# Two blocks of an output projection multiplied as a pair, with two of eight steps by seven products instead of eight

## The chip, the cores and the metric

The kernel runs on one core of one Trainium2 chip. The metric is the device time of the kernel in microseconds (us), the median of several runs. All data are float32.

## The reference

One layer of a hybrid decoder for 256 tokens of 2048 features. Two attention branches run on the same input, A (latent attention) and B (sliding window). Their outputs go through projections of their own, are gated, added and projected again; a gated feed-forward part follows. The part that matters here:

```python
merged = g[:, :, 0] * (o_a @ w_o_mla) + g[:, :, 1] * (o_b @ w_o_swa)
y = merged @ w_out
x = x + rms_norm(y, norm_mix_post)
```

`o_a` is 256 x 2048, `w_o_mla` and `w_out` are 2048 x 2048, `norm_mix_post` is the scale of 2048 numbers, and `g` are sigmoids of gate values.

## The kernel before, in words

**Products.** A float32 product is made of three matmuls in a reduced float32 type: every operand is split into a high and a low part, and `mm3` (L174) adds high by high, high by low and low by high into one PSUM bank (L175 to L177; the bank is 128 tokens by 512 columns). Activations stay in SBUF as pairs of tiles; two ktiles (128 rows of the contraction each) share one tile, so a product over 2048 rows has 16 ktiles in 8 ktile pairs. `AH`, `AL` are branch A's output (tiles `bhl0` to `bhl7`), `MH_`, `ML_` the merged values (`ahl0` to `ahl7`).

**Weights.** SP loads a chunk of 128 x 1024 into `raw` (up to five in flight), ScalarE casts it to the high part (`whi`, L143) and VectorE subtracts to get the low part (`wlo`, L144). High and low parts have rings of four buffers, so a conversion starts when TensorE has done with the chunk four before. `gemm` (L179) multiplies one block of 512 columns: 8 chunks of two ktiles, 12 matmuls each, with the two token halves in two banks.

**Pairs.** `pair_gemm` (L205) multiplies two blocks (1024 columns) at once into four banks, c11, c12, c21, c22 (token half by block). A "plain" ktile pair is multiplied as `gemm` would do it: 4 banks x 2 ktiles x 3, so 24 matmuls over two rows of weights of 1024 columns. A "seven" treats the 2 x 2 x 2 blocks of token halves, ktiles and column blocks by a scheme with seven products instead of eight: VectorE forms four sums of activation blocks (`token_sums`, L276) and four sums of weight blocks (L232 to L235), four of the products go to banks of their own (q1, q5, q7, q6), and behind the last seven VectorE adds these into four tiles d0 to d3 (L255 to L261), which the caller adds to c11 to c22. The two rows of weights of a seven are loaded by POOL's queue (L227, L228), the plain ones by SP's (L151). The kernel already multiplies a pair of gate blocks (`gate_pair`, L724, three sevens) and three pairs of the feed-forward part in this way.

**Steps.** Work that isn't on the main line is put on a calendar: `at(t, f)` runs f when `tick()` has counted t chunks; a scheduler then fixes the order on each engine. Each engine and each queue runs its instructions in order.

**Around the change.** Behind branch A's attention the four blocks of its gate were stored to DRAM (`ta_d`, L904) by POOL's queue, as were the gated blocks of branch B (`yb_d`). The loop at L950 to L958 then does, for each of four blocks j: POOL loads gate part `lta` (3 buffers) and `lyb` (2 buffers) from DRAM, one tile for each token half; `gemm` multiplies the block; VectorE merges, first (gate + 1) x product (L955), then + branch B (L956); and some chunks later TensorE transposes the merged block (`m_cols`, L930, tiles `mT`), which ScalarE and VectorE split into `ahl`. The accumulators come from the pool `pacc`, four banks taken in turn. The scale `gpost` (L917, L922) and the residual `x2` (L925) are loaded by SP during this loop, from chunk 10 on. The output product (L1013) follows, four blocks, of which the first uses the merged ktiles in order; `y_evac` (L969) reads the scale at L973. Two pools are opened ahead of the loop (`p6`, L916, and `px`, L927) over memory that the gate tiles (`ta`, `tb`) held.

Of the kernel before, what the change touches and what calls it, by code (L numbers as in the profile page):

```python
# [11 lines left out]
F32 = mybir.dt.float32  # L12
F32R = mybir.dt.float32r
# [3 lines left out]
ALU = mybir.AluOpType  # L17
AX = mybir.AxisListType

P = 128  # L20
D = 2048
S = 256
NT = 2
KT = D // P
# [17 lines left out]
def trunk_layer(ctx, tc, x, x_cols_in, conv_cols_in, g_mix_post, g_ffn_post, w_in, w_q, w_kv,  # L42
                sinks, rel, wo_a, wo_b, w_out, w_up, w_down, rope_tab, strip_sel, out):
    nc = tc.nc
    vec, act, pe, pool = nc.vector, nc.scalar, nc.tensor, nc.gpsimd
# [7 lines left out]
    pss = ctx.enter_context(tc.tile_pool(name="pss", bufs=2, space=PS))  # L53
# [5 lines left out]
    def sb(pl, shape, name, dt=F32, tag=None, bufs=None):  # L59
        return pl.tile(shape, dt, name=name, tag=tag or name, **({"bufs": bufs} if bufs else {}))  # L60
# [118 lines left out]
    def gemm(xh, xl, w, k0, nk, c0, n, split=None, extra=None, ps=None):  # L179

        kc = 1024 // n if n in (256, 512) else 2
        acc = new_acc("g", ps)
        todo = []
        cuts = list(range(0, nk, kc)) + [nk]
        for ci, (k, ke) in enumerate(zip(cuts[:-1], cuts[1:])):
            kk = ke - k
            src = w[(k0 + k) * P:(k0 + k + kk) * P, c0:c0 + n].rearrange("(a p) n -> p a n", p=P)
            hi, lo = wchunk(src, [kk, n], *(extra or {}).get(ci, ()))
            for j in range(kk):
                kt = k + j  # L190
# [473 lines left out]
    acc, _ = gemm(XH, XL, w_in, 0, KT, 0, 512)  # L664
# [4 lines left out]
    acc, _ = gemm(XH, XL, w_in, 0, KT, C_KV, KVR + ROPE)  # L669
# [21 lines left out]
    ta_d = dram.tile([4, NT, P, 512], F32, name="ta_d")  # L691
    yb_d = dram.tile([4, NT, P, 512], F32, name="yb_d")
# [55 lines left out]
    AH, AL = pair_view(ath), pair_view(atl)  # L748
# [138 lines left out]
    b = now[0] + 26  # L887
# [9 lines left out]
    at_ = [slot("b", p) for p in range(8)]  # L897
    ath[:], atl[:] = highs(at_), lows(at_)
    for j in range(4):
        acc, _ = gemm(XH, XL, w_in, 0, KT, C_GA + 512 * j, 512)  # L900
# [13 lines left out]
    x2_all = [sb(p3, [P, D], f"x2_{t}") for t in range(NT)]  # L914
    x2 = [[x_[:, j * 512:(j + 1) * 512] for j in range(4)] for x_ in x2_all]
    es6, p6 = open_pool("p6")  # L916
    gpost = sb(p6, [P, D], "gpost", tag="gp")  # L917

    def late_loads(i):

        if i < 4:
            nc.sync.dma_start(gpost[:, i * 512:(i + 1) * 512], g_mix_post[i * 512:(i + 1) * 512].partition_broadcast(P))  # L922
        else:
            t, j = divmod(i - 4, 4)
            nc.sync.dma_start(x2[t][j], x[t * P:(t + 1) * P, j * 512:(j + 1) * 512])  # L925

    esx, px = open_pool("px", bufs=EXTRA)  # L927
    es4, p4 = open_pool("p4")

    def m_cols(p, ld):  # L930
        pt = pst.tile([P, 512], F32, name=f"mT{p}", tag="t")
        for i in range(2):
            for t in range(NT):
                c = (2 * (p % 2) + i) * P
                pe.transpose(pt[:, i * 256 + t * P:i * 256 + (t + 1) * P], ld[t][0][:, c:c + P], ident)
        split_to(mth[p][:, :], mtl[p][:, :], pt, 0.5)

    def merge_loads(j):
        ld = []
        for t in range(NT):  # L940
            a = sb(p4, [P, 512], f"lta{j}_{t}", tag="lta", bufs=3)
            b = sb(p4, [P, 512], f"lyb{j}_{t}", tag="lyb", bufs=2)
            pool.dma_start(a, ta_d[j, t])
            pool.dma_start(b, yb_d[j, t])
            ld.append((a, b))
        return ld

    for i in range(12):
        at(now[0] + 10 + 2 * i, lambda i=i: late_loads(i))
    for j in range(4):  # L950
        ld = merge_loads(j)
        acc, _ = gemm(AH, AL, wo_a, 0, KT, 512 * j, 512)
        for t in range(NT):
            a, b = ld[t]
            vec.scalar_tensor_tensor(a, a, 1.0, acc[t], op0=ALU.add, op1=ALU.mult)  # L955
            vec.tensor_tensor(a, a, b, op=ALU.add)  # L956
        for p in range(2):
            at(now[0] + (3 if j == 3 else 1) + p, lambda p=2 * j + p, ld=ld: m_cols(p, ld))  # L958


    yg_all = [[sb(p6, [P, 1024], f"yg_{t}_{j}", tag="f" + "ab"[t], bufs=2) for j in range(2)] for t in range(NT)]
    yg = [[yg_all[t][j // 2][:, (j % 2) * 512:(j % 2 + 1) * 512] for j in range(4)] for t in range(NT)]
# [6 lines left out]
    def y_evac(acc, b, t):  # L969
        c0, n = W_BLOCKS[b]  # L970
        j, o = c0 // 512, c0 % 512
        act.activation(jk(f"yj{b}_{t}")[:, :n], acc[t][:, :n], AF.Square, accum_out=ssy[t][:, b:b + 1])
        vec.tensor_tensor(yg[t][j][:, o:o + n], acc[t][:, :n], gpost[:, c0:c0 + n], op=ALU.mult)  # L973

    x2hl = [slot("b", p) for p in range(8)]
    HH, HL = pair_view(highs(x2hl)), pair_view(lows(x2hl))
# [36 lines left out]
    for b in range(4):  # L1013
        c0, n = W_BLOCKS[b]
        last = b == 3
        acc, todo = gemm(MH_, ML_, w_out, 0, KT, c0, n, split=0 if last else None, extra={i: (px,) for i in range(EXTRA)} if last else None)
# [263 lines left out]
    ud = []  # L1280
# [5 lines left out]
    def pair_end(i):  # L1286
# [10 lines left out]
    for j in range(2, 4):  # L1297
        last = j == 3
        acc, todo = down(24, 20, 512 * j, 512, split=5 if last else None, ps=None if last else (pss, "s"))
# [25 lines left out]
RING = 4  # L1325
GATE_ORDER = "psppspsp"
B_ORDER = "pppsppspsp"
PAIR_ORDER = ("psppsppsppsp", "ppsppsppsppp")
XCUT = [0, 1, 2, 3, 4, 6, 8, 10, 12, 14, 16]
X_LOAD = [0, 1, 2, 3, 4, 6, 7, 8, 10]  # L1330
# [72 lines left out]
```

## Time and profile before

| what | value |
|---|---|
| time, median of 3 runs | 1468.54 us (1467.81 to 1469.31) |
| the profiled execution: its own time | 1470.05 us |
| its span, first to last instruction | 1468.3 us |
| TensorE busy | 1456.9 us, 99% |
| VectorE busy | 1067.2 us, 73% |
| ScalarE busy | 830.5 us, 57% |
| DMA | 287.60 MB, 196 GB/s on average |
| chain that ended last | TensorE 97% |

The profile is of one execution. Times in its rows count from the start of the span. A row of the timeline has the start, the duration, the engine, the line of the kernel, the operation, and the tiles (output<-inputs) without their numbers; in brackets stands how long the engine was idle before, and what ended that. Matmuls are pipelined: the duration of one holds its latency, and the distance of two starts says what it costs. PE is TensorE, PEld its weight load, DVE VectorE, ACT ScalarE; SPq is the DMA queue of SP.

### The profile page before, as it was taken

Reading aid. Unit: us, or ns where it says so; the run is one execution under the profiler, and the core shown is the slowest. Engines: PE = TensorE matmul, PEld = TensorE weight load, DVE = VectorE, ACT = ScalarE, POOL = GpSimd, SP = SyncE. Lnnn points to the kernel's source line nnn. Section 1 sums busy time; section 2 is a strip of 40 time slices with the busy share of each in tenths; the row PEclk is TensorE's granted clock in tenths of the full one; section 3 lists DMA queues with packets and bytes.
Section 4 is the critical chain, followed back from the end, with each engine's and each line's share of the span. In section 5 each row is a group of like instructions: output and inputs, shape, how many; then the busy total and the mean of one; then the engine's idle time right before and its main releaser. Section 6 shows DMA issues by size and latency. Waiting matters only on the chain.

```text
span 1468.3 us, 20938 instructions
## 1 busy us (share of the span) xinstructions
PE 1456.9 (99%) x7576; PEld 1244.8 (85%) x7576; DVE 1067.2 (73%) x1881; ACT 830.5 (57%) x1372; POOL 64.9 (4%) x113
## 2 busy tenths in 40 slices
PE   9999999999999999999999999999999999999997
PEld 7888888888888888888888888888888888888886
DVE  7688896745667665555699976778776687677775
ACT  7588874543555554444566655555454565555453
POOL 0011110000000000000000000000000000000000
PEclk9999999999999999999999999999999999999999
DMA  8755376466655559756766666665656666667573
GB/s 297 211 164 167 108 259 192 162 212 200 191 156 160 164 163 334 226 184 212 225 205 185 188 193 193 187 187 187 218 174 213 198 187 189 187 197 233 163 237 129
DMA packets 149909, 287.60 MB, mean 196 GB/s; under 512 B 18428, under 2 KB 29597, under 8 KB 149677
## 3 DMA queue, kind: packets, MB, share of 16 engines
q1 hardware_dynamic: 141312, 256.80, 56.5%
q0 software_dynamic: 8400, 29.41, 6.4%
q8 instruction: 59, 0.97, 0.3%
q14 instruction: 46, 0.37, 0.1%
q10 hardware_dynamic: 92, 0.05, 0.0%
HBM read 277.79 MB, written 8.44 MB: 195 GB/s over the span
## 4 chain that ended last, share of the span: by engine, by line
PE 97%; DVE 2%; ACT 1%; issue 0%; DMA 0%; DVEq 0%; ACTq 0%
PE accg L175 13%; PE accg L177 13%; PE accg L176 13%; PE ub L1147 10%; PE ua L1147 10%; PE ua L1151 5%; PE ub L1151 5%; PE cd L177 2%; PE cd L175 2%; PE cd L176 2%; PE cdb L175 1%; PE cdb L177 1%; PE cdb L176 1%; PE mpo L875 1%; PE cg L176 1%; PE cg L177 1%
## 5 line engine op out<-in xcount | busy, mean ns | idle before, releaser
L144 DVE TENSOR_TENSOR wlo<-raw,whi 128x1024 fp32r<-128x1024 f32 (+2 forms) x476 | 576.3, 1214 | 282.5 <-ACT whi L143 275.2
L143 ACT CAST whi<-raw 128x1024 fp32r<-128x1024 f32 (+2 forms) x476 | 494.7, 1043 | 427.5 <-PE accg L177 172.3
L175 PE MATMUL accg<-whi,ahl 128*128 128x512 f32 (+1 forms) x480 | 187.9, 392 | 0.0
L177 PE MATMUL accg<-whi,ahl 128*128 128x512 f32 (+1 forms) x480 | 185.6, 387 | 0.0
L176 PE MATMUL accg<-wlo,ahl 128*128 128x512 f32 (+1 forms) x480 | 184.8, 385 | 0.0
L1147 PE MATMUL ua<-ahl,whi 128*128 128x512 f32 x640 | 154.6, 391 | 0.0
L1147 PE MATMUL ub<-ahl,whi 128*128 128x512 f32 x640 | 154.6, 391 | 0.0
L175 PE MATMUL accg<-whi,bhl 128*128 128x512 f32 x378 | 148.2, 392 | 0.0
L177 PE MATMUL accg<-whi,bhl 128*128 128x512 f32 x378 | 147.4, 390 | 0.0
L176 PE MATMUL accg<-wlo,bhl 128*128 128x512 f32 x378 | 147.3, 390 | 0.0
L1147 PEld LDWEIGHTS ub<-ahl,whi 128*128 128x128 f32 x640 | 117.5, 188 | 22.9 <-ACT cc L1045 0.2
L1147 PEld LDWEIGHTS ua<-ahl,whi 128*128 128x128 f32 x640 | 117.6, 188 | 22.7
L177 PEld LDWEIGHTS accg<-whi,ahl 128*128 128x128 f32 x480 | 90.1, 188 | 18.0
L176 PEld LDWEIGHTS accg<-wlo,ahl 128*128 128x128 f32 x480 | 90.3, 188 | 15.6
L175 PEld LDWEIGHTS accg<-whi,ahl 128*128 128x128 f32 x480 | 90.3, 188 | 15.5
L1151 PEld LDWEIGHTS ub<-ahl,wlo 128*128 128x128 f32 x640 | 82.2, 191 | 3.2
L1151 PEld LDWEIGHTS ua<-ahl,wlo 128*128 128x128 f32 x640 | 82.2, 191 | 3.1
L1151 PE MATMUL ua<-ahl,wlo 128*128 128x256 f32 x640 | 83.7, 283 | 0.0
L177 PEld LDWEIGHTS accg<-whi,bhl 128*128 128x128 f32 x378 | 71.0, 188 | 14.8
L176 PEld LDWEIGHTS accg<-wlo,bhl 128*128 128x128 f32 x378 | 71.0, 188 | 14.5
L1151 PE MATMUL ub<-ahl,wlo 128*128 128x256 f32 x640 | 83.2, 283 | 0.0
L175 PEld LDWEIGHTS accg<-whi,bhl 128*128 128x128 f32 x378 | 71.0, 188 | 14.3
(545 smaller groups left out, 2218.9 us busy)
## 6 DMA issues: line engine op xcount, KB each, us to landing
raw<-in_ffn_w_up_dram SPq DMA_DIRECT2D x176, 512.0 KB, 4.5
raw<-in_w_in_dram SPq DMA_DIRECT2D x105, 512.0 KB, 4.5
raw<-in_ffn_w_down_dram SPq DMA_DIRECT2D x68, 512.0 KB, 4.5
raw<-in_w_o_swa_dram SPq DMA_DIRECT2D x32, 512.0 KB, 4.4
raw<-in_w_o_mla_dram SPq DMA_DIRECT2D x32, 512.0 KB, 4.5
raw<-in_w_out_dram SPq DMA_DIRECT2D x32, 512.0 KB, 4.1
bias<-strip POOLq DMA_DIRECT2D x16, 256.0 KB, 4.4
raw<-in_mla_w_q_up_dram SPq DMA_DIRECT2D x32, 128.0 KB, 2.8
```

What stands on the lines that cost most here:

```text
L143: act.copy(hi[:, a:b], raw[:, a:b])
L144: vec.tensor_tensor(lo[:, a:b], raw[:, a:b], hi[:, a:b].bitcast(F32), op=ALU.subtract)
L175: pe.matmul(o, ah, bh, start=start, stop=False)
L176: pe.matmul(o, ah, bl, start=False, stop=False)
L177: pe.matmul(o, al, bh, start=False, stop=stop)
L875: pe.matmul(o, w(t), p_[:, c], start=n == 0, stop=n == 5)
L1147: pe.matmul(acc[i], hi[:, c], hn[p][:, j * 512:(j + 1) * 512], start=p + j == 0, stop=stop)
L1151: pe.matmul(acc[i][:, 0:256], lo[:, c], hn[p][:, j * 512:j * 512 + 256], start=False, stop=False)
```

## The change

Blocks 1 and 2 of branch A's projection are multiplied as a pair; blocks 0 and 3 stay single. `A_ORDER` has the sevens at the fourth and the seventh place of eight; they take ktile pairs 0 and 1, so the plain ones begin with pair 2. The token sums are made during block 0 (calendar 1 and 4). The two sevens' weights go into the scale's tile and into `px`, and the scale is loaded during block 3 instead of from chunk 10 on. `lta` has a fourth buffer. The first parts `lta` of both blocks are loaded ahead of the pair, `lyb` of block 1 too, and `lyb` of block 2 in a step of its own, one chunk into block 3. At the pair's end VectorE adds each c to its d and merges. Block 3 takes its accumulators from the pool `pss`, whose banks q1 and q5 had.

```diff
     es6, p6 = open_pool("p6")
-    gpost = sb(p6, [P, D], "gpost", tag="gp")
+    gpost = []
...
         if i < 4:
-            nc.sync.dma_start(gpost[:, i * 512:(i + 1) * 512], g_mix_post[i * 512:(i + 1) * 512].partition_broadcast(P))
+            if i == 0:
+                gpost.append(sb(p6, [P, D], "gpost", tag="gp"))
+            nc.sync.dma_start(gpost[0][:, i * 512:(i + 1) * 512], g_mix_post[i * 512:(i + 1) * 512].partition_broadcast(P))
...
-    def merge_loads(j):
+    def merge_loads(j, kinds="ab"):
...
+            for kind, tag, src, bufs in (("a", "lta", ta_d, 4), ("b", "lyb", yb_d, 2)):
+                if kind in kinds:
+                    both.append(sb(p4, [P, 512], f"{tag}{j}_{t}", tag=tag, bufs=bufs))
+                    pool.dma_start(both[-1], src[j, t])
...
-    for i in range(12):
-        at(now[0] + 10 + 2 * i, lambda i=i: late_loads(i))
-    for j in range(4):
+    as_ = {}
+
+    def a_sums(u):
+        st = sb(px, [P, 1024], f"as{u}", F32R, tag="w" + ("hi", "lo")[u % 2])
+        tmp = sb(p6, [P, 1024], f"at{u}", tag="f" + "ab"[u % 2], bufs=2)
+        as_[u] = token_sums(at_[u].bitcast(F32), tmp[:, 0:512], tmp[:, 512:1024], st[:, 0:512], st[:, 512:1024])
+
+    def merged(a, b, acc):
+        vec.scalar_tensor_tensor(a, a, 1.0, acc, op0=ALU.add, op1=ALU.mult)
+        vec.tensor_tensor(a, a, b, op=ALU.add)
...
+    def a_place():
+        a_done[0] += 1
+        i = a_done[0]
+        if i % 2:
+            both = sb(p6, [P, D], f"ar{i}", tag="gp")
+            return both[:, 0:1024], both[:, 1024:2048]
+        return [sb(px, [P, 1024], f"ar{i}{n}", tag="w" + n) for n in ("hi", "lo")]
...
+    def f_pair(name):
+        return [sb(p6, [P, 1024], f"{name}{n}{cnt[0]}", tag="f" + n, bufs=2) for n in "ab"]
...
+    def single(j):
         ld = merge_loads(j)
-        acc, _ = gemm(AH, AL, wo_a, 0, KT, 512 * j, 512)
+        acc, _ = gemm(AH, AL, wo_a, 0, KT, 512 * j, 512, ps=(pss, "s") if j == 3 else None)
         for t in range(NT):
-            a, b = ld[t]
-            vec.scalar_tensor_tensor(a, a, 1.0, acc[t], op0=ALU.add, op1=ALU.mult)
-            vec.tensor_tensor(a, a, b, op=ALU.add)
+            merged(*ld[t], acc[t])
...
+    def a_pair():
+        lds = [merge_loads(1), merge_loads(2, "a")]
+        c = pair_gemm("a", wo_a, 0, 512, A_ORDER, lambda k, t: (AH(k)[:, t * P:(t + 1) * P], AL(k)[:, t * P:(t + 1) * P]),
+                      lambda u: as_[u], 0, ud_place, a_place, lambda: f_pair("ta"))
+
+        def pair_evac(i):
+            t, j = divmod(i, 2)
+            vec.tensor_tensor(ud_a[i], ud_a[i], c[i], op=ALU.add)
+            merged(*lds[j][t], ud_a[i])
+
+        def second_b():
+            for t, (b,) in enumerate(merge_loads(2, "b")):
+                lds[1][t].append(b)
+
+        for n_, i in zip((0, 1, 3, 4), (0, 2, 1, 3)):
+            at(now[0] + n_, lambda i=i: pair_evac(i))
+        at(now[0] + 1, second_b)
+        for p in range(2, 6):
+            at(now[0] + 1 + p, lambda p=p: m_cols(p, lds[p // 2 - 1]))
+
+    for u in range(A_ORDER.count("s")):
+        at(now[0] + 1 + 3 * u, lambda u=u: a_sums(u))
+    for i in range(4, 12):
+        at(now[0] + 10 + 2 * i, lambda i=i: late_loads(i))
+    single(0)
+    a_pair()
+    for i in range(4):
+        at(now[0] + i, lambda i=i: late_loads(i))
+    single(3)
...
+A_ORDER = "pppsppsp"
```

How this moves instructions, at the three places that the prediction speaks of. First VectorE's queue in block 0, before: the conversions of block 0's last chunks (353 to 361) and of block 1's first (363 to 367) stand next to each other, then come the merges.

```order
L144 TENSOR_TENSOR wlo_5930<-raw_5927,whi_5929 128x1024
L144 TENSOR_TENSOR wlo_5948<-raw_5945,whi_5947 128x1024
L144 TENSOR_TENSOR wlo_5966<-raw_5963,whi_5965 128x1024
L144 TENSOR_TENSOR wlo_5984<-raw_5981,whi_5983 128x1024
L144 TENSOR_TENSOR wlo_6002<-raw_5999,whi_6001 128x1024
L144 TENSOR_TENSOR wlo_6034<-raw_6031,whi_6033 128x1024
L144 TENSOR_TENSOR wlo_6052<-raw_6049,whi_6051 128x1024
L144 TENSOR_TENSOR wlo_6077<-raw_6074,whi_6076 128x1024
L955 SCALAR_TENSOR_TENSOR lta_0_5863<-lta_0_5863,accg_346_0_5871 128x512
```

The same place now, the beginning (the first token sum, L278 to L284, in tiles `at0` and `as0`, and the second in `at1`) and the end (the weight sums of the second seven, L232 to L235, and the first merge, now L959):

```order
L144 TENSOR_TENSOR wlo353_5938<-raw352_5935,whi353_5937 128x1024
L278 TENSOR_TENSOR at0_5909<-bhl0_4096 128x512
L144 TENSOR_TENSOR wlo355_5956<-raw354_5953,whi355_5955 128x1024
L281 TENSOR_TENSOR at0_5909<-at0_5909 128x128
...
L144 TENSOR_TENSOR wlo363_6057<-raw362_6054,whi363_6056 128x1024
L233 TENSOR_TENSOR taa386_6303<-ar2lo_6300,ar2hi_6299 128x512
L234 TENSOR_TENSOR tab386_6304<-ar2lo_6300,taa386_6303 128x512
L144 TENSOR_TENSOR wlo365_6075<-raw364_6072,whi365_6074 128x1024
L235 TENSOR_TENSOR tab386_6304<-ar2lo_6300,tab386_6304 128x512
L144 TENSOR_TENSOR wlo367_6100<-raw366_6097,whi367_6099 128x1024
L959 SCALAR_TENSOR_TENSOR lta0_0_5862<-lta0_0_5862,accg_346_0_5870 128x512
```

Between the conversion of chunk 353 and the merge stand now 27 operations instead of 7: both token sums and all eight weight sums of the two sevens have come in between. Second, POOL's queue, now, from the sevens' weights (`ar1`, `ar2hi`, `ar2lo`) on:

```order
L904 DMA ta_d_2539<-ta3_1_5835 128x512
L227 DMA ar1_6176<-in_w_o_mla_dram 128x1024
L228 DMA ar1_6176<-in_w_o_mla_dram 128x1024
L227 DMA ar2hi_6299<-in_w_o_mla_dram 128x1024
L228 DMA ar2lo_6300<-in_w_o_mla_dram 128x1024
L947 DMA lyb1_0_6040<-yb_d_2540 128x512
...
L947 DMA lyb3_0_6393<-yb_d_2540 128x512
L947 DMA lyb3_1_6397<-yb_d_2540 128x512
L947 DMA lta3_0_6391<-ta_d_2539 128x512
L947 DMA lta3_1_6395<-ta_d_2539 128x512
L947 DMA lyb2_0_6446<-yb_d_2540 128x512
```

The sevens' four rows go out right behind the last gate write; `lyb` of block 3 goes out ahead of `lyb` of block 2, which takes the same buffers. Third, TensorE's queue at the head of the output product (`accg_410`, chunk 415 is its third), now:

```order
L175 MATMUL accg_410_0_6618<-whi415_6659,ahl2_5845 128x512
L176 MATMUL accg_410_0_6618<-wlo415_6660,ahl2_5845 128x512
L937 MATMUL mT4_6547<-ident_76,lta2_0_6046 128x128
L937 MATMUL mT5_6573<-ident_76,lta2_0_6046 128x128
L177 MATMUL accg_410_0_6618<-whi415_6659,ahl2_5845 128x512
L175 MATMUL accg_410_1_6619<-whi415_6659,ahl2_5845 128x512
L176 MATMUL accg_410_1_6619<-wlo415_6660,ahl2_5845 128x512
L937 MATMUL mT4_6547<-ident_76,lta2_1_6048 128x128
```

Before, the transposes of block 2 (`mT4`, `mT5`) stood behind the second and the third chunk of block 3; now they stand 26 matmuls into the output product, inside its third chunk, ahead of those of block 3.

More of the change, by code (lines that the diff above doesn't have):

```diff
@@ L936, in m_cols @@
         split_to(mth[p][:, :], mtl[p][:, :], pt, 0.5)
-    def merge_loads(j):
+    def merge_loads(j, kinds="ab"):
         ld = []
         for t in range(NT):
[L941 to L945, printed above, removed]
-        return ld
-    for i in range(12):
-        at(now[0] + 10 + 2 * i, lambda i=i: late_loads(i))
@@ L950, in trunk_layer @@
-    for j in range(4):
+            both = []
+            for kind, tag, src, bufs in (("a", "lta", ta_d, 4), ("b", "lyb", yb_d, 2)):
+                if kind in kinds:
+                    both.append(sb(p4, [P, 512], f"{tag}{j}_{t}", tag=tag, bufs=bufs))
+                    pool.dma_start(both[-1], src[j, t])
+            ld.append(both)
+        return ld
+    as_ = {}
[3 more added lines that the diff above has]
+        as_[u] = token_sums(at_[u].bitcast(F32), tmp[:, 0:512], tmp[:, 512:1024], st[:, 0:512], st[:, 512:1024])
@@ new lines, in merged @@
+    def merged(a, b, acc):
+        vec.scalar_tensor_tensor(a, a, 1.0, acc, op0=ALU.add, op1=ALU.mult)
+        vec.tensor_tensor(a, a, b, op=ALU.add)
+    a_done = [0]
+    def a_place():
[5 more added lines that the diff above has]
+        return [sb(px, [P, 1024], f"ar{i}{n}", tag="w" + n) for n in ("hi", "lo")]
+    ud_a = []
+    def f_pair(name):
+        return [sb(p6, [P, 1024], f"{name}{n}{cnt[0]}", tag="f" + n, bufs=2) for n in "ab"]
@@ L951, in trunk_layer, with ud_place @@
+    def ud_place():
+        ud_a[:] = [x_[:, j * 512:(j + 1) * 512] for x_ in f_pair("ud") for j in range(2)]
+        return ud_a
+    def single(j):
         ld = merge_loads(j)
-        acc, _ = gemm(AH, AL, wo_a, 0, KT, 512 * j, 512)
+        acc, _ = gemm(AH, AL, wo_a, 0, KT, 512 * j, 512, ps=(pss, "s") if j == 3 else None)
         for t in range(NT):
-            a, b = ld[t]
-            vec.scalar_tensor_tensor(a, a, 1.0, acc[t], op0=ALU.add, op1=ALU.mult)
-            vec.tensor_tensor(a, a, b, op=ALU.add)
+            merged(*ld[t], acc[t])
@@ L972, in y_evac @@
         act.activation(jk(f"yj{b}_{t}")[:, :n], acc[t][:, :n], AF.Square, accum_out=ssy[t][:, b:b + 1])
-        vec.tensor_tensor(yg[t][j][:, o:o + n], acc[t][:, :n], gpost[:, c0:c0 + n], op=ALU.mult)
+        vec.tensor_tensor(yg[t][j][:, o:o + n], acc[t][:, :n], gpost[0][:, c0:c0 + n], op=ALU.mult)
     x2hl = [slot("b", p) for p in range(8)]
```

## The prediction

> **What bounds the kernel now.** I read the page first (busy time, then the chain that ended last), then the busy time by stretch.
>
> ```profile
> span 1468.3 us, 20938 instructions
> PE 1456.9 (99%) x7576; PEld 1244.8 (85%) x7576; DVE 1067.2 (73%) x1881; ACT 830.5 (57%) x1372; POOL 64.9 (4%) x113
> PE 97%; DVE 2%; ACT 1%; issue 0%; DMA 0%; DVEq 0%; ACTq 0%
> ```
>
> TensorE is busy for 1456.9 of 1468.3 us and holds 97% of the chain. Only two things can move the time here: TensorE's own work, and waits put in front of it. The busy time of four stretches (TensorE, weight load, VectorE, ScalarE, POOL; then clock, DMA share, GB/s) shows what there is to win:
>
> ```profile
> 242.70:284.70 42.00, 42.00 (x185) 34.28 (x184) 29.31 (x32) 21.91 (x23) 2.17 (x4) 1.00 0.44 148
> 553.40:575.10 21.70, 21.70 (x97) 17.97 (x96) 10.00 (x9) 9.16 (x10) 1.09 (x2) 1.00 0.91 330
> 575.10:643.30 68.20, 68.20 (x313) 56.39 (x312) 39.94 (x43) 29.22 (x31) 5.90 (x11) 1.00 0.71 232
> 643.30:666.00 22.70, 22.70 (x105) 18.79 (x104) 13.91 (x15) 9.84 (x11) 0.00 (x0) 1.00 0.68 225
> ```
>
> The first stretch is a pair with three sevens that the kernel already has (the gates); the next two are block 0 and blocks 1 to 3 of the projection that is changed; the last is the first block of the output product. TensorE is never idle in any of them. So the projection has no idle time to give back, the form with sevens can run without a gap, and VectorE has room on average (39.94 of 68.20 us).
>
> **The change part by part.**
>
> *Products.* Each seven leaves out one of eight 512-column products, three matmuls; two sevens leave out six. Start to start of matmuls in the old block 1:
>
> ```profile
> 589.00 0.39 PE L175 MATMUL accg<-whi,bhl 128*128 128x512 f32 x1
> ...
> 599.88 0.39 PE L175 MATMUL accg<-whi,bhl 128*128 128x512 f32 x1
> ```
>
> Between these are 48 matmuls: 10.88 / 48 = 0.227 us each (the 0.39 us duration is latency and overlaps). Six of them are **-1.36 us**. That is the whole gain; everything else can only cost.
>
> *VectorE's new work.* Its pace, in rows where it doesn't wait (start to start):
>
> ```profile
> 213.17 0.28 DVE L281 TENSOR_TENSOR xm<-xa 128x128 f32<-128x128 f32 x1
> 213.38 0.28 DVE L282 TENSOR_TENSOR xm<-xa 128x128 f32<-128x128 f32 x1
> ...
> 645.42 2.36 DVE L144 TENSOR_TENSOR wlo<-raw,whi 128x1024 fp32r<-128x1024 f32 x2
> ...
> 1023.15 0.69 DVE L232 TENSOR_TENSOR ta<-rr 128x512 f32<-128x512 f32 x1
> 1023.75 0.69 DVE L233 TENSOR_TENSOR ta<-rr 128x512 f32<-128x512 f32 x1
> ```
>
> So 0.21 us for 128 columns, 0.60 us for 512, 2.36/2 = 1.2 us for a conversion (1.14 where the next follows at once). New are two token sums (2 x 2.0 us), eight weight sums (4.8), 1.5 more conversions in each seven than in the two plain rows it replaces (3.4), four adds in the last seven and four where the pair is put together (4.8): 17 us in a stage that leaves VectorE 11.7 + 28.3 us. By amount it is hidden behind TensorE. What matters is two places where TensorE waits for one particular VectorE instruction.
>
> *Place 1, the start of the pair.* The pair holds four accumulator banks. Its third product goes into the bank of block 0's first accumulator, which is freed by block 0's first merge (L955, now L959). Before, block 1 took the other two banks, and that merge had 22 us. Ahead of the merge VectorE now has both token sums and all weight sums, and the first token sum writes the first tile of a new pool, over memory that the gate tiles used. The trace shows what such a first write waits for; there it was the scale's load on SP:
>
> ```profile
> 553.85 1.23 POOL L904 DMA_DIRECT2D ta_d<-ta  x2 [2.86 <-ACT ta L903]
> ```
> ```profile
> SPq L922 <- DMA ta_d<-ta: 2.7, 1, 2.7
> ```
> ```profile
> 559.88 0.34 SPq L922 DMA_DIRECT2D gpost<-in_norm_mix_post_dram  x1
> ```
>
> It waited 2.7 us for the last gate write to land, and went at 559.9. The change moves this wait from SP, where it cost nothing, to VectorE; I take its end as 559.7. Behind it on VectorE, up to the merge: 7 conversions, 12 operations of 512 columns and 8 of 128, 7 x 1.14 + 12 x 0.60 + 8 x 0.205 = 16.8 us, so the merge starts at 576.5 and, at half of the 1.28 us for two below, ends at 577.2. Before:
>
> ```profile
> 573.68 1.23 DVE L144 TENSOR_TENSOR wlo<-raw,whi 128x1024 fp32r<-128x1024 f32 x1 [1.49 <-ACT whi L143]
> 574.82 1.28 DVE L955 SCALAR_TENSOR_TENSOR lta<-lta,accg 128x512 f32<-128x512 f32 x2
> ```
> ```profile
> 575.11 0.39 PE L175 MATMUL accg<-whi,bhl 128*128 128x512 f32 x1
> ...
> 576.47 0.39 PE L175 MATMUL accg<-whi,bhl 128*128 128x512 f32 x1
> ```
>
> 575.11 is the first matmul of block 1, 576.47 the seventh, which in the pair is the first into the bank that the merge frees. TensorE would wait 577.2 - 576.5 = 0.7 us and a tenth for the signal: **+0.8 us**. The conversions among these are late too, but by the same sum the last three end at 572.5, 574.8 and 576.6, for products that begin at 575.1, 577.8 and 580.5, so nothing waits for them. The lower bound is zero (if the wait is elsewhere, VectorE starts the sums at 556.4, right behind the conversion of 555.21, and keeps up). The upper bound comes from the sevens' weights, which POOL now loads in one burst, 4 x 512 KB, and which wait for the same write (559.9). The gates' burst is the nearest row:
>
> ```profile
> L227 POOL DMA_DIRECT2D gr<-in_w_in_dram x2: 528/546/564, 200.7 to 201.8; - x2
> ...
> DMA to landing us min/median/max: 4.0/5.4/7.7
> ```
>
> By its first, 4.0 us, the first row is there at 563.9; VectorE asks for it at 559.7 + 3 x 0.60 + 8 x 0.205 + 2 x 1.14 = 565.4. By the last, 7.7 us, it lands at 567.6, 2.2 us late, which the merge passes on: 3.0 us. I take the burst's first, since the row asked for is the first issued.
>
> *Place 2, the head of the output product.* Block 2's second gate part (lyb) is now loaded into the buffers that block 3's part holds, so POOL issues it only behind block 3's merge, and the transposes of block 2 stand among the first matmuls of the output product, 26 behind its start. The rows of an equal step of before, with 575.11 as the start of the next product:
>
> ```profile
> 576.01 1.29 DVE L956 TENSOR_TENSOR lta<-lta,lyb 128x512 f32<-128x512 f32 x2
> ```
> ```profile
> 577.00 1.15 POOL L944 DMA_DIRECT2D lyb<-yb_d  x2 [21.92 <-DVE lta L956]
> ```
> ```profile
> L944 POOL DMA_DIRECT2D lyb<-yb_d x8: 537/539/544, 548.9 to 623.1; - x8
> ...
> DMA to landing us min/median/max: 3.1/4.2/6.0
> ```
>
> POOL issues 577.00 - 575.11 = 1.9 us behind the start, the load lands 4.2 us later (the median), a tenth for the signal, and one add of 0.69 us: 6.9 us. TensorE is there after 26 x 0.227 = 5.9 us. It waits **+1.0 us**; with 3.1 us nothing, with 6.0 us 2.8 us. Behind the waiting add stands the conversion of the seventh chunk, which is needed 6 x 12 x 0.227 = 16 us into the product, so nothing more.
>
> The Trainium skill, "DMA: Bandwidth & Descriptors", section "Anatomy of one DMA", puts such a transfer at about 2.0 us and its bytes at 436 GB/s. By an estimate from that page 256 KB land in 2.6 us, and this wait would be gone; the rows' least is 3.1 us and their median 4.2, so I go by the rows.
>
> *The rest.* At the pair's end the second bank of block 3 is freed by the last of the seven's adds: VectorE has two conversions and four adds up to there, 2 x 1.14 + 4 x 0.60 = 4.7 us from about the end of the last seven, TensorE a plain pair and one product, 27 x 0.227 = 6.1 us: hidden, with 1.4 us to spare, and one for one beyond.
>
> ```profile
> 666.28 1.43 DVE L973 TENSOR_TENSOR yg<-accg,gpost 128x512 f32<-128x512 f32 x2
> ```
>
> The scale's four loads move from 560 to behind the first seven's weights, 6 x 12 x 0.227 = 16 us and more into the pair, and are first read at 666: nothing. On SP they stand ahead of the last plain row, whose product is 20 us off (a seven, two plain pairs and a seven, 90 matmuls). Two token splits and one copy on ScalarE (57% busy) cost nothing.
>
> **Sum** -1.36 + 0.8 + 1.0 = +0.4 us. The profiled execution took 1470.05 us in all (its span and 1.8 us around it), which becomes 1470.5; it lies 1.5 us above the median of the three runs, 1468.54, so the forecast is **1469.0 us**.
>
> **The rivals.**
> - *Waits covered.* The first token sum needn't wait, or lyb lands in 3.1 us. Both: 1467.2; one alone: 1468.0 to 1468.2. For it: in the gates' stretch TensorE lost nothing. Against: there the accumulators before the pair were in other banks. 28%.
> - *Slower: late weights at place 1.* The four loads meet x's loads in the same 12 us of a DMA that already moves 330 GB/s. From a first landing 5.5 us after the issue each further us reaches TensorE through the merge. With 7.7 us: -1.36 + 3.0 + 1.0 = +2.6, 1471.2; with lyb at 6.0 us too, +4.4, 1473.0. For it: the second half of the gates' burst took 6.1 to 7.7 us. Against: it is the first that counts. 20%. The Trainium skill, "TensorE: Matmul & The Clock Gate", section "HAM oscillation", warns of TensorE gaps above some 3.4 us, after which the clock drops. By that rule no single wait here is long enough; the row below shows a clock at full, and a gap that long isn't in this stage.
>
> ```profile
> core 0: 1468.3 us, clock 0.998
> ```
>
> - *Faster than the products.* Moving the scale's loads would have to end a TensorE wait; the stretches show none. 3%.
>
> **How the numbers follow.** Forecast (both waits, 0 to +1.5) 45%, covered 28%, late weights 20%, a wait in the sevens or at the pair's end that I priced at nothing 4%, faster 3%. The range runs from both waits covered, 1467.2 less the 0.6 us by which runs differ, to late weights with part of a slow lyb: 1466.6 to 1472.0. A difference of 0.2% (2.9 us) is about what a measurement of this kernel can tell from no change; beyond it on the slow side lie late weights with more than their single price, 9%, and the unpriced wait, 4%, on the fast side 3%; within it 84%.
>
> **What would show it.** In the changed profile: 0.227 us between matmuls in the pair, and 21 of them in a seven; a VectorE wait for the gate write ahead of the first L278 near 556 to 560; a gap of TensorE of 0.8 us ahead of the seventh matmul of the pair, and one of 1.0 us ahead of the first transpose of block 2, some 6 us into the output product. I am wrong if TensorE waits in the sevens themselves, if the burst's first row lands after 565, or if a gap appears that starts behind 666 us.

## The result, and the profile after

The changed kernel took 1474.31 us (median of 6 runs, 1473.28 to 1476.64) against 1468.87 us before (6 runs, 1467.81 to 1469.31). The ratio is 1.0042, with a 95% interval of 1.0031 to 1.0052: **5.4 us slower**, 2.3 us outside the range given.

From the page of the changed kernel, the span, the busy times and the first row of the chain:

```profile
span 1472.8 us, 20960 instructions
PE 1457.0 (99%) x7570; PEld 1244.5 (85%) x7570; DVE 1083.3 (74%) x1913; ACT 835.4 (57%) x1379; POOL 67.0 (5%) x117
PE 89%; issue 5%; DVE 3%; DMA 1%; ACT 1%; POOL 0%; DVEq 0%; ACTq 0%; POOLq 0%
```

TensorE has the six matmuls less (7576 to 7570) and VectorE 16 us more work, where 17 were forecast. The waits of TensorE for other engines (us in total, times, longest) say where the time went:

```profile
PE mT L937 <- DVE lta L960: 3.0, 1, 3.0
PE ca L175 <- DVE lta L959: 3.0, 1, 3.0
PE warm L77 <- DVE ramp L66: 1.1, 1, 1.1
PE pstrip L349 <- DMA sel<-in_strip_sel_dram: 0.2, 1, 0.2
```

The last two rows, at the start of the kernel, were there before as well. The first two are new, and they are the two waits that the prediction named: the pair's first matmul into the bank of block 0's first merge (place 1), and the first transpose of block 2 (place 2). Each was taken for a third of what it is, or less.

This execution runs 1.18 us ahead of the old one where block 0 ends (573.93 for the first matmul behind it, where it was 575.11), and it is 5.16 us behind at the last matmul (1464.53 where it was 1459.37): the stage costs 6.3 us here. The two spans differ by 4.5 only because of that head start and a tail that is 0.7 us shorter. Place 1 in the rows of the timeline, TensorE first:

```profile
575.07 0.39 PE L177 MATMUL ca<-whi,bhl 128*128 128x512 f32 x1
578.41 0.50 PE L175 MATMUL ca<-whi,bhl 128*128 128x512 f32 x1 [2.96 <-DVE lta L959]
578.75 0.39 PE L176 MATMUL ca<-wlo,bhl 128*128 128x512 f32 x1
```

From start to start that is 3.34 us where 0.227 is the pace, and 0.34 for the next: **3.2 us lost**. Place 2:

```profile
648.70 0.39 PE L176 MATMUL accg<-wlo,ahl 128*128 128x512 f32 x1
652.09 0.66 PE L937 MATMUL mT<-ident,lta 128*128 128x128 f32 x2 [3.00 <-DVE lta L960]
652.40 0.78 PE L177 MATMUL accg<-whi,ahl 128*128 128x512 f32 x1
652.97 0.63 PE L175 MATMUL accg<-whi,ahl 128*128 128x512 f32 x1
653.40 0.63 PE L176 MATMUL accg<-wlo,ahl 128*128 128x512 f32 x1
653.83 1.42 PE L937 MATMUL mT<-ident,lta 128*128 128x128 f32 x6
654.96 0.52 PE L177 MATMUL accg<-whi,ahl 128*128 128x512 f32 x1
655.31 0.40 PE L175 MATMUL accg<-whi,ahl 128*128 128x512 f32 x1
```

Here 3.2 us pass without a matmul, and then the matmuls themselves are slow: 0.43 us from one to the next instead of 0.227, up to 655. Start to start these rows add about another 1.6 us: **4.8 us lost**. The stretches around both places (busy time of the five engines, then the granted clock, DMA share and GB/s) tell why:

```profile
575.00:578.40 3.40, 0.45 (x3) 0.03 (x1) 3.40 (x5) 1.25 (x2) 0.00 (x0) 1.00 1.03 399
578.40:582.00 3.60, 3.59 (x16) 3.00 (x17) 3.60 (x5) 1.06 (x1) 1.09 (x2) 1.00 0.96 373
649.00:651.60 2.60, 0.09 (x1) 0.00 (x0) 1.10 (x2) 1.04 (x1) 0.00 (x0) 1.00 0.79 245
651.60:655.00 3.40, 2.91 (x12) 2.55 (x12) 2.17 (x3) 0.30 (x1) 0.00 (x0) 0.50 0.69 248
655.00:660.00 5.00, 5.00 (x26) 4.19 (x25) 2.52 (x3) 2.54 (x4) 0.00 (x0) 1.00 0.33 107
```

The granted clock is 0.50 from 651.6 to 655.0 and 1.00 on either side; behind place 1 it stays at 1.00. The sum of the rows, -1.36 + 3.2 + 4.8 = 6.6, meets the 6.3 us of the stage within 0.3.

### The profile page after: what moved, and what is told of

Read it like the earlier page. It is cut to its first block, busy times and chain, and to the rows that moved or that the text cites. A ratio compares the mean times of both kernels' runs of the same rounds, so it can differ in the third digit from the quotient of the medians.

```text
span 1472.8 us, 20960 instructions
## 1 busy us (share of the span) xinstructions
PE 1457.0 (99%) x7570; PEld 1244.5 (85%) x7570; DVE 1083.3 (74%) x1913; ACT 835.4 (57%) x1379; POOL 67.0 (5%) x117
## 4 chain that ended last, share of the span: by engine, by line
PE 89%; issue 5%; DVE 3%; DMA 1%; ACT 1%; POOL 0%; DVEq 0%; ACTq 0%; POOLq 0%
PE accg L175 10%; PE accg L177 10%; PE accg L176 10%; PE ub L1206 10%; PE ua L1206 10%; PE ub L1210 5%; PE ua L1210 5%; PE cd L176 2%; PE cd L175 2%; PE cd L177 2%; PE cdb L176 1%; PE cdb L175 1%; PE cdb L177 1%; PE mpo L875 1%; PE cg L176 1%
## 5 line engine op out<-in xcount | busy, mean ns | idle before, releaser
L175 PE MATMUL accg<-whi,bhl 128*128 128x512 f32 x314 | 122.9, 391 | 0.0
L177 PE MATMUL accg<-whi,bhl 128*128 128x512 f32 x314 | 122.4, 390 | 0.0
L176 PE MATMUL accg<-wlo,bhl 128*128 128x512 f32 x314 | 122.4, 390 | 0.0
L177 PEld LDWEIGHTS accg<-whi,bhl 128*128 128x128 f32 x314 | 59.0, 188 | 12.3
L175 PEld LDWEIGHTS accg<-whi,bhl 128*128 128x128 f32 x314 | 59.0, 188 | 12.0
L176 PEld LDWEIGHTS accg<-wlo,bhl 128*128 128x128 f32 x314 | 59.0, 188 | 11.9
```

The costliest lines, as they stand in the source:

```text
L175: pe.matmul(o, ah, bh, start=start, stop=False)
L176: pe.matmul(o, ah, bl, start=False, stop=False)
L177: pe.matmul(o, al, bh, start=False, stop=stop)
```

## The experiments

The theory (A) from these rows: two waits and a slowed clock, nothing else; the six products less are gained in full. The main rival (B): the sevens' work on VectorE and their weights make the stage late as such, and whatever wait is taken away comes back at another place. The kernel before took 1468.5 to 1468.7 us beside these runs.

**Block 0 in other banks.** Block 0 accumulates in the two banks of `pss`, so the pair doesn't need its merge.

```diff
-        acc, _ = gemm(AH, AL, wo_a, 0, KT, 512 * j, 512, ps=(pss, "s") if j == 3 else None)
+        acc, _ = gemm(AH, AL, wo_a, 0, KT, 512 * j, 512, ps=(pss, "s") if j in (0, 3) else None)
```

> Block 0 accumulates in two banks of the score pool, so that the pair's four banks are free before block 0's first merge; the rest as in the changed kernel (1474.3 us). Theory A (two waits and a slowed clock behind the second make up the loss: 3.2 us at the pair's start, 3.2 us ahead of the transposes of block 2, 1.6 us by the clock): the wait ahead of the pair's seventh matmul goes, 1471.1 us; the wait at place 2 stays at about 3.0. Rival B (the sevens' work on VectorE and their weights are late as such, and the bank only shows it): the next product of the pair waits instead, 1473.5 to 1474.3 us.

Measured: 1470.92 us (1469.95 to 1472.35), ratio 1.0017 (1.0008 to 1.0026). The wait for `lta` L959 is gone from TensorE's waits, that for L960 stays at 2.8. Theory A met it; place 1 is worth 3.4 us.

**Second gate parts in the other order.** Block 2's `lyb` is loaded ahead of block 3's.

```diff
-        ld = merge_loads(j)
+        ld = merge_loads(j, "a" if j == 3 else "ab")
+        if j == 3:
+            def third_b():
+                for t, (b,) in enumerate(merge_loads(3, "b")):
+                    ld[t].append(b)
+
+            at(now[0] + 5, third_b)
```

> Block 2's second gate part is loaded ahead of block 3's, which takes its buffers later; the rest as in the changed kernel (1474.3 us). Theory A: the wait ahead of the first transpose of block 2 goes, and with it the half clock behind it: 1474.3 - 3.2 - 1.6 = 1469.5 us. Rival B (the first chunks of the output product are late in any case, since the merge of block 3 is): TensorE waits some 2 us at the same place for block 3's part or for a converted chunk: 1471.5 to 1472.7 us. Rival C (the slow matmuls are not the clock's answer to the gap): 1471.1 us with slow matmuls still there.

Measured: 1471.34 us (1468.44 to 1474.63), ratio 1.0018 (1.0009 to 1.0027). In its trace the wait of place 2 is gone, the clock is 1.00 throughout, and only 2.3 us of wait at place 1 are left. The mechanism is A's, but the median is 1.8 us above A's number: the time of place 1 alone varies over 6 us from run to run. B's wait is ruled out by the trace, not by this median, and the trace is of an execution of 1469.51 us, near the low end.

**Both.**

> Both edits, the bank of block 0 and the order of the second gate parts. Theory A: both waits and the slow clock go, and six products less are left: 1474.3 - 3.2 - 4.8 = 1466.3 us, or 1468.9 - 1.4 = 1467.5 us counted from the kernel before; 1466.0 to 1467.6. Rival B (another wait takes their place): 1468.5 us or more.

Measured: 1467.46 us (1466.57 to 1468.74), ratio 0.9991 (0.9982 to 0.9999). TensorE waits nowhere in the stage:

```profile
PE warm L77 <- DVE ramp L66: 1.1, 1, 1.1
PE acckv L415 <- ACT whi L143: 0.9, 1, 0.9
PE pstrip L349 <- DMA sel<-in_strip_sel_dram: 0.4, 1, 0.4
```

All three are at the start of the kernel. That refutes rival B and gives the prices a second time, in medians: place 1 alone 1471.34 - 1467.46 = 3.9 us, place 2 alone 1470.92 - 1467.46 = 3.5 us (4.8 in the one trace above), both 1474.31 - 1467.46 = 6.85 us; and without either the kernel is **1.2 us faster** than the one before. These are the six products: from block 0's first matmul to one in the second block of the output product this trace takes 665.32 - 552.85 = 112.47 us, the one before took 667.18 - 553.35 = 113.83, 1.36 us more.

**x loaded later.** What makes VectorE late at place 1? The eight loads of x are held back behind block 0's merge.

```diff
             merged(*ld[t], acc[t])
+            if j == 0:
+                vec.tensor_copy(x2_all[t][:, 0:D:512], ld[t][0][:, 0:4])
```

> The eight loads of x, 2 MB, are held back behind block 0's merge by a copy of four columns into each of their tiles; the rest as in the changed kernel (1474.3 us). Theory A1 (the sevens' weights land late because x's loads share the DMA with them): the first weights land in 4 to 5 us instead of 6.9, VectorE's 1.7 us of waits for weights go, the wait ahead of the seventh matmul falls from 3.1 to about 1.4: 1472.6 us. Rival A2 (the wait for the gate write and VectorE's added work alone make it): landing and wait as before, 1474.3 us.

Measured: 1471.99 us (1469.62 to 1475.15), ratio 1.0024 (1.0015 to 1.0033), 2.3 us less than the changed kernel. VectorE up to the first merge, rows of this run:

```profile
565.00 0.69 DVE L232 TENSOR_TENSOR taa<-ar 128x512 f32<-128x512 f32 x1
567.34 0.69 DVE L233 TENSOR_TENSOR taa<-ar 128x512 f32<-128x512 f32 x1
576.15 1.28 DVE L959 SCALAR_TENSOR_TENSOR lta<-lta,accg 128x512 f32<-128x512 f32 x2
```

and of the changed kernel:

```profile
559.04 0.69 DVE L278 TENSOR_TENSOR at<-bhl 128x512 f32<-128x512 f32 x1 [3.78 <-DMA ta_d<-ta]
566.13 0.69 DVE L232 TENSOR_TENSOR taa<-ar 128x512 f32<-128x512 f32 x1 [1.31 <-DMA ar<-in_w_o_mla_dram]
568.83 0.69 DVE L233 TENSOR_TENSOR taa<-ar 128x512 f32<-128x512 f32 x1 [0.27 <-DMA ar<-in_w_o_mla_dram]
577.68 1.28 DVE L959 SCALAR_TENSOR_TENSOR lta<-lta,accg 128x512 f32<-128x512 f32 x2
```

Without x's loads the sevens' first row lands in 5.0 us instead of 6.9, both waits for weights are gone, the merge is 1.5 us earlier, and TensorE's wait is 1.6 us instead of 3.0. From its first token sum (559.29) to the merge VectorE now has 16.9 us without a wait for a load. A1 holds for 1.4 us of the wait; the gate write and VectorE's added work make the other 1.6, so A2 holds for no more than that. The time fell by 2.3 us, not by 1.4; in this trace the clock also stays at 1.00 behind place 2, which may be the rest.

**Sevens' weights loaded later.** The other way to clear VectorE's queue ahead of the merge: each of the sevens' weight tiles is first written by a copy that needs block 0's merged tile.

```diff
+    a_first, at0_ld = [], []
...
             both = sb(p6, [P, D], f"ar{i}", tag="gp")
+            vec.tensor_copy(both[:, 0:D:1024], a_first[0][:, 0:2])
             return both[:, 0:1024], both[:, 1024:2048]
-        return [sb(px, [P, 1024], f"ar{i}{n}", tag="w" + n) for n in ("hi", "lo")]
+        ws = [sb(px, [P, 1024], f"ar{i}{n}", tag="w" + n) for n in ("hi", "lo")]
+        for w_ in ws:
+            vec.tensor_copy(w_[:, 0:2], a_first[0][:, 0:2])
+        return ws
...
+        if j == 0:
+            at0_ld[:] = [x_[0] for x_ in ld]
...
     single(0)
+    a_first[:] = at0_ld
```

> The sevens' weights are loaded only behind block 0's merge (a copy of two columns into each of their tiles holds the loads back), so that the eight weight sums leave the stretch ahead of the merge; the first token sum and its wait for the gate write stay. The rest as in the changed kernel (1474.3 us). Theory A1 (the weight sums and their late landing make VectorE late): from 559.0 VectorE has 7 conversions, 4 sums of 512 and 8 of 128 columns, 12.0 us, and is done at 571, ahead of the merge's earliest time: the wait of place 1 goes, 1470.9 us, as with the other bank (1470.9). Rival A2 (the wait for the gate write is what counts): 3 us stay at place 1, 1474 us. Rival A3 (the weights, 16 us later, are now late for the first seven): a new wait some 16 us into the pair, 1472 us or more.

Measured: 1474.38 us (1473.85 to 1475.07), ratio 1.0038 (1.0023 to 1.0054). No time is won, and the waits show why:

```profile
PE mT L937 <- DVE lta L960: 3.2, 1, 3.2
PE qa L176 <- DVE wlo L144: 2.4, 1, 2.4
```

```profile
559.21 0.69 DVE L278 TENSOR_TENSOR at<-bhl 128x512 f32<-128x512 f32 x1 [3.83 <-DMA ta_d<-ta]
573.77 1.27 DVE L959 SCALAR_TENSOR_TENSOR lta<-lta,accg 128x512 f32<-128x512 f32 x2
585.72 0.69 DVE L232 TENSOR_TENSOR taa<-ar 128x512 f32<-128x512 f32 x1 [3.11 <-DMA ar<-in_w_o_mla_dram]
588.21 0.69 DVE L233 TENSOR_TENSOR taa<-ar 128x512 f32<-128x512 f32 x1 [1.80 <-DMA ar<-in_w_o_mla_dram]
```

The token sum waits for the gate write as long as ever, yet the merge is 3.9 us earlier and place 1 is gone. That is A1 as it is put for this run, the eight weight sums and the landing of their weights together. But the weights, sent for at 577.8, now come too late for the first seven, which waits 2.4 us (A3), with half a clock behind it. The wait was moved, not removed.

**No sevens.** The pair with eight plain ktile pairs.

```diff
-            vec.tensor_tensor(ud_a[i], ud_a[i], c[i], op=ALU.add)
-            merged(*lds[j][t], ud_a[i])
+            merged(*lds[j][t], c[i])
...
-A_ORDER = "pppsppsp"
+A_ORDER = "pppppppp"
```

> The pair with eight plain ktile pairs and no seven: no token or weight sums, no loads of weights by POOL, the banks and the second gate parts as in the changed kernel (1474.3 us). Theory A: without the sums VectorE is at block 0's merge in time as before, the wait of place 1 goes (3.4), six products come back (+1.4), place 2 stays with 3.0 to 4.8: 1471.7 to 1473.3 us. Rival B (the pair's banks alone cost the wait at place 1): 1475.7 us.

Measured: 1472.34 us (1471.62 to 1473.18), ratio 1.0024 (1.0014 to 1.0035), in theory A's range. Place 1 is gone, though the banks are those of the changed kernel: the bank is only where VectorE's lateness shows. Place 2 is there with 2.2 us and half a clock.

**Fewer conversions ahead of block 3's merge.** Place 2 was forecast with the merge at 0.3 us ahead of the output product; it stands 1.7 us behind it. VectorE's queue has one converted chunk of the output product more ahead of it than before, 417 (before, it stood behind the merges):

```
L144 TENSOR_TENSOR wlo413_6642<-raw412_6639,whi413_6641 128x1024
L144 TENSOR_TENSOR wlo417_6678<-raw416_6675,whi417_6677 128x1024
L144 TENSOR_TENSOR wlo415_6660<-raw414_6657,whi415_6659 128x1024
L959 SCALAR_TENSOR_TENSOR lta3_0_6391<-lta3_0_6391,accg_394_0_6399 128x512
```

The ring of converted weights gets a fifth buffer for the output product, which lets that conversion start a chunk earlier; giving it that buffer one block of the product later puts 417 behind the merge. On top of block 0's other banks:

```diff
-    flex[0] = "w"
-    turn.update(raw=0, w=0)
     for b in range(4):
+        if b == 1:
+            flex[0] = "w"
+            turn.update(raw=0, w=0)
```

> As the run with the other bank for block 0 (1470.9 us, a wait of 2.9 us at place 2), but the weight ring changes its shape one product later, so that only two converted chunks of the output product's next ones, not three, stand ahead of block 3's merge on VectorE. Theory D1 (place 2 is longer than forecast because that third conversion, with its wait for its raw chunk, puts the merge 2.0 us late): the merge starts 0.3 us ahead of the output product and not 1.8 behind it, the wait at place 2 falls from 2.9 to about 1.0, the clock stays full behind it: 1467.5 + 1.0 = 1468.5, 1468.0 to 1469.2 us. Rival D2 (the landing of block 2's part alone makes it): wait and time as before, 1470.9 us.

Measured: 1468.73 us (1467.25 to 1470.59), ratio 1.0001 (0.9992 to 1.001), 2.2 us less than with the banks alone. VectorE in the run with the banks alone (output product's first matmul at 640.09):

```profile
639.60 2.36 DVE L144 TENSOR_TENSOR wlo<-raw,whi 128x1024 fp32r<-128x1024 f32 x2 [2.44 <-ACT whi L143]
641.88 1.28 DVE L959 SCALAR_TENSOR_TENSOR lta<-lta,accg 128x512 f32<-128x512 f32 x2
```

and in this run (first matmul at 639.07):

```profile
638.78 1.28 DVE L959 SCALAR_TENSOR_TENSOR lta<-lta,accg 128x512 f32<-128x512 f32 x2
644.22 1.28 DVE L960 TENSOR_TENSOR lta<-lta,lyb 128x512 f32<-128x512 f32 x2
```

The merge went from 1.8 us behind the product's start to 0.3 us ahead of it, as D1 has it, and the wait of place 2 is gone altogether in this trace, since `lyb` landed in 3.0 us here and in 4.0 there: 2.1 us of the change are the merge's, 1.0 the landing's, which may be the new ring's doing or chance. The median lies 1.3 us above that of the run with both edits, about the 1.0 us of wait that D1 left; that other executions still have it is argued, not seen (the trace also has a TensorE wait of 0.7 us far outside the stage, at 1064.7 us).

**The clock.** On the kernel with the second gate parts in the other order, block 0's first merge is done in two operations, with the other half's merge between them, so that place 1 lasts longer.

```diff
-            merged(*ld[t], acc[t])
+            if j == 0 and t == 0:
+                a, b = ld[t]
+                vec.tensor_tensor(a, a, acc[t], op=ALU.mult)
+                vec.tensor_tensor(a, a, acc[t], op=ALU.add)
+                vec.tensor_tensor(a, a, b, op=ALU.add)
+            else:
+                merged(*ld[t], acc[t])
```

> As the run with the second gate parts in the other order (median 1471.3, range 1468.4 to 1474.6), but block 0's first merge is done in two operations with the second merge between them, so that its bank comes free 1.2 us later: the wait of place 1 becomes 1.2 us longer, about 4 us. Theory C1 (a TensorE gap near 3 us and more halves the granted clock for 3.4 us): the rows behind the gap show 0.50, and the time is 1471.3 + 1.2, and up to 1.7 more, 1472.5 to 1474.2 us. Rival C2 (the clock's fall belongs to place 2 alone): 1.00 throughout, 1472.5 us.

Measured: 1471.90 us (1468.58 to 1473.86), ratio 1.0017 (1.0009 to 1.0026). The trace has a wait of 3.7 us at place 1, and half a clock behind it:

```profile
575.00:579.50 4.50, 0.84 (x4) 0.38 (x2) 4.50 (x7) 1.85 (x2) 0.00 (x0) 1.00 1.03 397
579.50:580.90 1.40, 1.38 (x6) 1.16 (x7) 1.40 (x3) 0.00 (x0) 0.00 (x0) 1.00 1.01 373
580.90:584.20 3.30, 3.30 (x10) 2.54 (x9) 2.70 (x3) 1.05 (x1) 1.08 (x2) 0.51 0.85 292
584.20:586.00 1.80, 1.80 (x11) 1.51 (x10) 0.00 (x0) 0.45 (x1) 0.00 (x0) 0.95 0.71 214
```

So the clock can fall behind place 1 too, against C2. The time doesn't decide between them: 0.6 us above the run it builds on, where 1.2 was the least, and both runs spread over more than 5 us.

**The changed kernel again.**

> The changed kernel once more, for the spread of its time and for a second profile. Theory C (waits of 2.4 to 3.4 us sometimes bring the half clock and sometimes don't): 1474.3 us median again, a spread of 3 us or more where the kernel without the two waits spread over 2.2 us (1466.6 to 1468.7), and a profile in which the half clock may stand at the other place, at both or at none. Rival (each wait always does the same): place 1 with 1.00 and place 2 with 0.50 again, spread 1.5 us like the kernel before.

Measured: 1474.39 us (1473.63 to 1478.26), ratio 1.0046 (1.0033 to 1.006). The spread is C's, the profile the rival's: 2.7 us of wait at place 1 with the clock at 1.00 behind it, 2.6 us at place 2 with 0.51 for 3.4 us, as the first time. What decides can be read from the traces (last section).

**Three sevens.** On the kernel with both edits, to see whether the form without waits has more to give. First `A_ORDER = "ppspspsp"`:

> Both edits (bank and order of the second gate parts, 1467.5 us) with three sevens instead of two, the first one ktile pair earlier. Theory: three products less, 1467.5 - 0.7 = 1466.8 us. Rival (VectorE, which now has the sums of three sevens in the same stretch, makes TensorE wait): 1467.5 us or more, with a wait for a converted half of a seven.

Measured: 1472.75 us (1470.42 to 1474.9), ratio 1.0027 (1.0017 to 1.0037). TensorE waits 3.3 us in the first seven (`qa<-wlo`). Then, with the first seven later, `A_ORDER = "pppspssp"`:

> Both edits with three sevens, the first one again behind three plain ktile pairs, the other two one behind the other (the run with the first seven behind two plain pairs took 1472.8 us, with 3.3 us of wait for the second half of the first seven). Theory: the first seven's sums have 5 us more, no TensorE wait in it, three products less than with two sevens: 1467.5 - 0.7 = 1466.8 us. Rival: the third seven's weights, loaded into the tile that the first one frees, hold VectorE's queue up again, and TensorE waits 1 us or more: 1468 us or more.

Measured: 1468.96 us (1467.56 to 1472.33), ratio 1.0005 (0.9996 to 1.0014), with 2.0 us at the same matmul. VectorE there:

```profile
593.77 0.69 DVE L232 TENSOR_TENSOR taa<-ar 128x512 f32<-128x512 f32 x1 [2.95 <-DMA ar<-in_w_o_mla_dram]
594.95 0.69 DVE L233 TENSOR_TENSOR taa<-ar 128x512 f32<-128x512 f32 x1 [0.49 <-DMA ar<-in_w_o_mla_dram]
595.56 1.22 DVE L144 TENSOR_TENSOR wlo<-tab,whi 128x1024 fp32r<-128x1024 f32 x1
```

The third seven's first sums wait for their weights, and behind them in the queue stands the conversion that the first seven needs. The rival was right both times. The best of all runs stays the pair with two sevens and both edits, 1467.46 us.

## Why the prediction was wrong, point by point

- *Products, -1.36 us:* right. The kernel without the two waits is 1.2 us faster than the one before, 0.1 to 2.6 us by its interval, and in its trace the stage is 1.36 us shorter.
- *Place 1, +0.8 us:* the mechanism was right, the size wrong; 3.2 us in the trace, 3.4 and 3.9 us by medians. VectorE's own work from the first token sum to the merge, 16.8 us in the forecast, was right: 577.68 - 559.04 = 18.6 us hold 1.6 us of waits for weights. The mis-sized term is the weights' landing. "I take the burst's first", 4.0 us, because the gates' burst had it; the row asked for first took 6.9 us, in a DMA that was at a share of 0.83 in these 6.9 us and of 0.96 in their last four, with x's loads in it; with these held back it took 5.0, at 0.68. The threshold given, 5.5 us, was right (6.9 less 5.5 is 1.4), and this is the rival "late weights" that had 20%. The rest is the gate write's end: the token sum starts at 559.04, not 559.7, but TensorE runs 1.18 us ahead here, so it comes half a microsecond later than taken. 0.7 + 1.6 + 0.5 = 2.8 of the 3.0 us. The run with x's loads held back shows the cause of the 1.6.
- *Place 2, +1.0 us:* the mechanism was right, one term was wrong. The landing of `lyb`, taken as 4.2 us, was 4.3 for the token half that TensorE waited for. The step "POOL issues 577.00 - 575.11 = 1.9 us behind the start" failed: POOL issued 3.9 us behind the product's start, since block 3's merge was 2.0 us late. One converted chunk more had moved ahead of it; the order of VectorE's queue has that row, and I took the merge's place from an equal step of before instead of reading it. The run with the ring changed later shows it. The rows of the changed kernel:

```profile
643.03 0.39 PE L175 MATMUL accg<-whi,ahl 128*128 128x512 f32 x1
644.72 1.28 DVE L959 SCALAR_TENSOR_TENSOR lta<-lta,accg 128x512 f32<-128x512 f32 x2
646.89 1.14 POOL L947 DMA_DIRECT2D lyb<-yb_d  x2 [10.65 <-DVE lta L960]
651.25 0.69 DVE L960 TENSOR_TENSOR lta<-lta,lyb 128x512 f32<-128x512 f32 x1 [1.50 <-DMA lyb<-yb_d]
```

- *The clock, nothing:* wrong, and the larger miss in kind. "By that rule no single wait here is long enough" took the Trainium skill's rule ("TensorE: Matmul & The Clock Gate", section "HAM oscillation", no TensorE gaps above some 3.4 us) as a lower bound for harm. Waits from 2.2 us on brought half the clock for 3.4 us, which cost about 1.6 us behind place 2; a wait of 3.2 us in the run with the late weights didn't. The traces disagree with the figure as a threshold for the length of a wait; what they follow instead is in the last section.
- *The rest, nothing:* right. No wait at the pair's end, in the sevens or for the scale; none starts behind 666 us.
- *The chances:* the rival that came true had 20%. With a slow `lyb` too it gave 1473.0, with waits of 3.0 and 2.8 us, near those measured, though the second came from a late issue and not from a slow landing. The range ended at 1472.0, and 9% stood for more than 0.2% on that side. The clock's 1.6 us stood in neither number.

For the Trainium skill's "DMA: Bandwidth & Descriptors", section "Anatomy of one DMA", 256 KB would land in an estimated 2.6 us; `lyb` of block 2 took 3.0 us in the run with the ring changed later and 3.5 to 4.5 in those where TensorE waited for it. The traces disagree with the estimate; what else the DMA carried (a share of 0.79 in the 3.0 us, of 0.89 in the 4.0 us of the run with the other banks) may be why, which no run tested.

## What to carry to other kernels

When a change puts work ahead of an instruction that TensorE waits for, read that instruction's whole queue in the new order, conversions that moved by themselves too, and price each load in it by what shares the DMA in those microseconds, not by the best row of another place. A TensorE wait of 2 to 3 us should be priced with a second term of up to 1.7 us (half of 3.41) for the clock behind it, with a chance: by an estimate from the limit in the next section, a wait that falls anywhere meets it in almost half of the cases at 2 us and in three quarters at 3 us. Before a cheaper product is given up, take away its waits one by one: here a change of one bank and one load's order turned 5.4 us lost into 1.2 us gained.

## What the runs showed of the hardware that was not expected

- *The clock behind a wait.* In the stage that was changed, thirteen TensorE waits of 2 us and more stand in ten traces. Behind seven of them the granted clock fell to 0.50 for some 3.4 us (waits of 2.2, 2.4, 2.6, 2.8, 3.0, 3.3 and 3.7 us), behind six it stayed at 1.00 (2.0, 2.3, 2.5, 2.7, 3.0 and 3.2 us). Its length alone doesn't decide: the fall came 2.5 us into the wait at place 2 of the changed kernel and 1.4 us after the end of the wait of 3.7 us. The traces show what does. From where a trace's record of the clock begins, at 1.00, to each fall the time is a whole number of spans of 3.413 us (in the changed kernel from 9.92 to 651.63 us, 188 of them; 167 to 188 in the seven traces), and these seven falls last one span each. Counted in these spans, TensorE's rows in all thirteen traces (the kernel before among them) follow one limit: up to the end of the matmuls the clock fell at the end of every span with 1.97 us or more without a matmul, and of none with 1.88 us or less. A wait that lies in one span meets the limit sooner than one that two spans share:

| run | TensorE wait, us | without a matmul, in each span, us | clock behind |
|---|---|---|---|
| no sevens, place 2 | 2.2 | 2.23 | 0.50 |
| changed kernel, place 2 | 3.0 | 2.54 and 0.46 | 0.50 |
| changed kernel, place 1 | 3.0 | 1.08 and 1.88 | 1.00 |
| late weights, place 2 | 3.2 | 1.66 and 1.56 | 1.00 |
| the run on the clock, place 1 | 3.7 | 1.71 and 1.97 | 0.50 |

  This is read off the traces; no run moved a wait against the spans to test it.
- *Spread.* The kernel without waits in this stage spread over 2.2 us in 11 runs, those with place 2 alone over 2.4 and (without sevens) 1.6; the five sets of runs with a wait at place 1 spread over 3.4 to 6.2 us. Each run leaves one trace, so what differs there from execution to execution was not seen. That the clock is part of it is likely: in the repeat of the changed kernel the mean granted clock was 0.997 in the three executions up to 1474.39 us, 0.996 in that of 1475.05 and 0.995 in that of 1478.26, and one fall takes 0.0012 off the mean.
- *A burst slows itself.* The sevens' four loads of 512 KB, issued by POOL 0.5 us apart, landed 6.9, 9.1, 11.0 and 12.8 us after their issues with x's loads beside them (the DMA moved 325 GB/s from 562 to 566 us and 412 from 566 to 570), and 5.0, 6.2, 7.5 and 11.0 us without.
